# Embedding norm and first kv projection: single token tiles or pairs of them

## The chip, the cores and the metric

One Trainium2 chip, one of its cores. The metric is the device time of one execution in microseconds (us): lower is better. The engines are named by their work: TensorE (PE in the rows; PEld is its weight load), VectorE (DVE), ScalarE (ACT), GpSimd (POOL) and SyncE (SP), which only issues transfers. L128 is line 128 of the kernel before.

## What is computed

A two-layer decoder trunk over 512 tokens of 2048 features, all in fp32. What matters here is its start: the embedding is normalised over its features, and the first thing that layer 0 needs of it is the 320 columns of `w_in` that hold the compressed keys and values (256) and the shared rotary key (64).

```python
def layernorm(x, g, b):
    xf = x.astype(jnp.float32)
    mu = jnp.mean(xf, axis=-1, keepdims=True)
    var = jnp.mean(jnp.square(xf - mu), axis=-1, keepdims=True)
    y = (xf - mu) * lax.rsqrt(var + LN_EPS) * g + b
...
h = layernorm(x, emb_ln_g, emb_ln_b)
for l in range(DEPTH):
    h = hybrid_layer(h, positions, w_in[l], ...)
# in hybrid_layer: proj = x @ w_in, split into q_lat, kv_lat, k_rope and the gates
```

Everything behind this (attention, pooling, convolution, output projection, the second layer) is the same program before and after.

## The kernel before

**Numbers in two parts.** An fp32 product is made of three TensorE passes: each operand is split into a high part (a ScalarE copy to fp32r) and a low part (the VectorE difference, L79 to L81), and `mm3` (L99 to L103) adds high x high, high x low and low x high. So a k-step of a projection for one token tile is three matmuls, and each weight block must be split before it is used.

**The opening** is the block from L205 to L299. The 512 tokens are four tiles of 128; `xr[t]` holds tile t as four chunks of 128x512. `load_x` (L212) issues a tile's four chunks on SyncE's queue. `normalise(t, on_act)` (L219) does four `bn_stats`, then `ln_stats` (L119: aggregate, add epsilon, and the power -0.5 on GpSimd, L124), then an offset, and normalises the chunks, the first `on_act` of them on ScalarE (L227), the others on VectorE (L128).

`ln_to_x` (L133) turns a normalised tile: for every group of `nk` of the 16 column blocks it makes TensorE transposes into one PSUM bank (L142), applies gain and bias in the bank (L149 on VectorE for even groups, L151 on ScalarE for odd ones), and splits the bank into XH (ScalarE, L80) and XL (VectorE, L81). Four banks (`bankB`) go around. The first tile goes in groups of four blocks, the others in groups of two.

The weights come in six units: `load_w` (L233) loads 3 x 128 rows of the 320 columns (the last unit 128), `split_w` (L238) makes the high part on ScalarE (L241) and the low part on GpSimd (L244; unit 4 on VectorE, units 2 and 3 in one piece, the others in thirds). `kv_proj` (L198) then runs 16 k-steps for the given tiles into `kv_ps[t]`, one PSUM bank each.

**The order of the work.** Each engine runs its own queue in order. The code names the work tile by tile (L277 to L297): tile 0 is normalised and turned, with the weight splits in between; then the projection of tile t is woven with the turning of tile t + 1 at listed k-steps (`weave`, L156). A list scheduler takes this order as priorities and puts on each engine's queue what it expects to be ready, so the queues need not have the written order. SyncE's queue has x of tile 0, the gain and bias rows `ve`, the constants `ct` (with the identity for transposes), weight units 0 and 1, x of tile 1, unit 2, x of tile 2, units 3 to 5, x of tile 3, and the small vectors of later stages (L255 to L272). At most eight transfers are out at a time: a later one is issued when the one eight places ahead of it has landed. At the end `spill` (L130) stores the normalised tiles.

The next stage is the q projection of layer 0 (`in_steps`, L167): 128x512 matmuls whose weights are loaded and split in the same way. Behind its first four k-steps the four kv tiles, evacuated in the meantime (L361 to L370), are turned by transposes (L392).

Of the kernel before, what the change touches and what calls it, by code (L numbers as in the profile page):

```python
# [10 lines left out]
F32 = mybir.dt.float32  # L11
# [8 lines left out]
P = 128  # L20
# [4 lines left out]
NT = T // P  # L25
# [28 lines left out]
def hybrid_trunk(ctx: ExitStack, tc: tile.TileContext, consts, x, positions, emb_ln_g, emb_ln_b,  # L54
# [13 lines left out]
    def bankA():  # L68
        return psA.tile([P, 512], F32, name="bankA", tag="bankA")
# [7 lines left out]
    xn_dram = dram.tile([T, D], F32, name="xn_dram")  # L77

    def split(hi, lo, src):  # L79
        nc.scalar.copy(hi, src)  # L80
        nc.vector.tensor_sub(lo, src, hi.bitcast(F32))  # L81

    def unit(src, shape, into=None):

# [34 lines left out]
    def ln_stats(sp, stats):  # L119
        mv = sp.tile([P, 2], F32, name="mv", tag="mv", bufs=4)  # L120
        nc.vector.bn_aggr(mv, stats)
        rstd = sp.tile([P, 1], F32, name="rstd", tag="rstd", bufs=4)
        nc.vector.tensor_scalar(rstd, mv[:, 1:2], 1.0, LN_EPS, op0=ALU.mult, op1=ALU.add)
        nc.gpsimd.tensor_tensor(rstd, rstd, half[:, 0:1], op=ALU.pow)  # L124
        return mv[:, 0:1], rstd
# [4 lines left out]
    def spill(t, r):  # L130
        nc.sync.dma_start(xn_dram[t * P:(t + 1) * P, :], r.rearrange("p c n -> p (c n)"))

    def ln_to_x(ts, rs, vg, vb, nk):  # L133

        n = len(ts)
        w = n * P
        for s in range(KT // nk):
            ps = bankB()
            for j in range(nk):
                k = nk * s + j  # L140
                for i in range(n):
                    nc.tensor.transpose(out=ps[:, (n * j + i) * P:(n * j + i + 1) * P],  # L142
                                        in_=rs[i][:, k // 4, (k % 4) * P:(k % 4 + 1) * P], identity=ident)
            for j in range(nk):
                k = nk * s + j
                g, b = vec[:, vg + k:vg + k + 1], vec[:, vb + k:vb + k + 1]
                src = ps[:, j * w:(j + 1) * w]
                if s % 2 == 0:
                    nc.vector.tensor_scalar(src, src, g, b, op0=ALU.mult, op1=ALU.add)  # L149
                else:  # L150
                    nc.scalar.activation(src, src, AF.Identity, bias=b, scale=g)  # L151
            kq = slice(nk * s, nk * (s + 1)), slice(ts[0] * P, ts[0] * P + w)
            split(XH[:, kq[0], kq[1]], XL[:, kq[0], kq[1]], ps[:, :nk * w].rearrange("p (j q) -> p j q", j=nk))
            yield

    def weave(main, side, at):  # L156

# [51 lines left out]
    with tc.tile_pool(name="start", bufs=1, reuse_waits="tile") as sp:  # L209
        xr = M01 + [sp.tile([P, 4, 512], F32, name=f"xr{i}", tag=f"xr{i}") for i in range(2)]  # L210

        def load_x(t):  # L212
            src = x[0, t * P:(t + 1) * P, :].rearrange("p (c n) -> p c n", c=4)
            for c in range(4):
                nc.sync.dma_start(xr[t][:, c, :], src[:, c, :])

        st = [sp.tile([P, 4, 6], F32, name=f"stats{t}") for t in range(NT)]

        def normalise(t, on_act):  # L219
            for c in range(4):  # L220
                nc.vector.bn_stats(st[t][:, c, :], xr[t][:, c, :])  # L221
            mu, rstd = ln_stats(sp, st[t])
            o = sp.tile([P, 1], F32, name=f"off{t}")
            nc.vector.scalar_tensor_tensor(o, in0=mu, scalar=-1.0, in1=rstd, op0=ALU.mult, op1=ALU.mult)
            for c in range(4):
                if c < on_act:
                    nc.scalar.activation(xr[t][:, c, :], xr[t][:, c, :], AF.Identity, bias=o, scale=rstd)  # L227
                else:
                    norm_chunk(xr[t], c, mu, rstd)

        raws, us = [], []

        def load_w(u):  # L233
            src, n = kv_block(0, u)
            raws.append(sp.tile([P, 3 * KVN], F32, name=f"kvraw{u}"))
            nc.sync.dma_start(raws[u][:, :n * KVN].rearrange("p (a b) -> p a b", a=n), src)

        def split_w(u):  # L238
            n = kv_block(0, u)[1]
            d = dp.tile([P, 2, 1024], F32R, name="dunit", tag="dunit") if u < 5 else kvx  # L240
            nc.scalar.copy(d[:, 0, :n * KVN], raws[u][:, :n * KVN])  # L241
            step = n * KVN if u in (2, 3) else KVN
            for a in range(0, n * KVN, step):
                (nc.vector if u == 4 else nc.gpsimd).tensor_sub(  # L244
                    d[:, 1, a:a + step], raws[u][:, a:a + step], d[:, 0, a:a + step].bitcast(F32))
            us.append(tuple(d[:, i, :n * KVN].rearrange("p (a b) -> p a b", a=n) for i in range(2)))

        def to_vec(tl, n, at):
            vps = bankB()
            nc.tensor.transpose(out=vps[:, :n], in_=tl, identity=ident[:n, :n])  # L250
            nc.vector.tensor_copy(vec[:, at:at + n], vps[:, :n])

        ve = sp.tile([V_LG, P], F32, name="ve")
        vr = sp.tile([V_N - V_LG, P], F32, name="vr")
        load_x(0)  # L255
        for row, v in ((V_EG, emb_ln_g), (V_EB, emb_ln_b)):
            nc.sync.dma_start(ve[row:row + 16, :], v.rearrange("(a p) -> a p", p=P))
        nc.sync.dma_start(ct, consts)
        load_w(0)
        load_w(1)  # L260
        load_x(1)
        load_w(2)
        load_x(2)
        load_w(3)
        load_w(4)
        load_w(5)
        load_x(3)
        for row, v in ((V_LG, ln_g[0]), (V_LB, ln_b[0])):
            nc.sync.dma_start(vr[row - V_LG:row - V_LG + 16, :], v.rearrange("(a p) -> a p", p=P))
        for row, n, v in ((V_QG, 8, q_norm_g), (V_KG, 4, kv_norm_g), (V_PS, 8, pool_scale)):  # L270
            nc.sync.dma_start(vr[row - V_LG:row - V_LG + n, :], v.rearrange("l (a p) -> (l a) p", p=P))
        nc.sync.dma_start(vr[V_CW - V_LG:, :], conv_w.rearrange("l w (a p) -> (l w a) p", p=P))  # L272
        kv_ps = [bankA() for _ in range(NT)]
        def turn_x(t, nk):
            return ln_to_x((t,), xr[t:t + 1], V_EG, V_EB, nk)

        normalise(0, 3)  # L277
        to_vec(ve, V_LG, 0)
        first = turn_x(0, 4)
        next(first)  # L280
        split_w(0)
        next(first)
        next(first)
        for u in (1, 2, 3):
            split_w(u)
        next(first)
        split_w(4)
        normalise(1, 4)
        split_w(5)
        weave(kv_proj(us, kv_ps, (0,)), turn_x(1, 2), (11, 13) + 6 * (15,))  # L290
        normalise(2, 4)
        normalise(3, 0)
        weave(kv_proj(us, kv_ps, (1,)), turn_x(2, 2), tuple(range(5, 13)))
        weave(kv_proj(us, kv_ps, (2,)), turn_x(3, 2), (10, 12, 14) + 5 * (15,))
        to_vec(vr, V_N - V_LG, V_LG)
        for _ in kv_proj(us, kv_ps, (3,)):
            pass  # L297
        for t in range(NT):
            spill(t, xr[t])  # L299

# [556 lines left out]
```

## Time and profile before

| | |
|---|---|
| median of 3 runs | 1459.86 us (1459.64 to 1459.88) |
| profiled execution | 1459.91 us, span 1458.0 us |
| TensorE busy | 1435.6 us, 98% of the span |
| VectorE, ScalarE, GpSimd busy | 729.1, 561.8 and 108.0 us |
| share of TensorE in the chain that ended last | 98% |

The span runs from the first instruction to the last; the time has some 2 us around it. Times in the rows are us from the span's start. A timeline row gives the start, the time from the start of its first to the end of its last instruction, engine, line, operation, written tile and read tiles, shapes, how many were merged (x4), and in square brackets the idle time of the engine ahead of it and what ended it. Neighbouring instructions of an engine overlap at their ends, so the spacing of the starts is what one costs its engine, and the length is what the next engine waits. On TensorE the lengths are modelled; the starts are not.

### The profile page before, as it was taken

The numbers are of one execution on the slowest core, as the hardware profiler recorded it, in microseconds if no ns is written. First come the engines' busy times: TensorE is split into PE (matmuls) and PEld (weight loads), VectorE is DVE, ScalarE is ACT, GpSimd is POOL, SyncE is SP. The second block draws the span as 40 slices with busy tenths as digits, with TensorE's granted clock in tenths as the row PEclk, the third lists the DMA queues.
The fourth block names the chain that finished last, engine by engine and source line by source line (L and its number), as shares of the span: only waits on it lengthen the run. The fifth ranks groups of instructions, "written<-read, shape, count | busy, mean of one in ns | idle before, by whom it ended". The sixth has DMA issues, their size and how long they took to land.

```text
span 1458.0 us, 18179 instructions
## 1 busy us (share of the span) xinstructions
PE 1435.6 (98%) x7202; PEld 1226.9 (84%) x7202; DVE 729.1 (50%) x1244; ACT 561.8 (39%) x882; POOL 108.0 (7%) x130
## 2 busy tenths in 40 slices
PE   6999999999999999999999999999999999999997
PEld 6988888888888888888998888888888888888897
DVE  7745666553233257534573365666432423583336
ACT  7645566542222234222254365555322122432123
POOL 3011000012000000000001100000200000000004
PEclk9999999999999999999999999999999999999999
DMA  8532222133333347333523232232333333553333
GB/s 287 147 92 66 79 80 79 50 111 96 92 102 89 100 125 265 102 101 103 172 88 108 66 94 59 66 87 63 104 101 101 88 101 101 189 201 102 100 132 116
DMA packets 131104, 160.51 MB, mean 110 GB/s; under 512 B 13920, under 2 KB 109388, under 8 KB 127948
## 3 DMA queue, kind: packets, MB, share of 16 engines
q1 hardware_dynamic: 131020, 159.36, 36.1%
q8 instruction: 56, 0.92, 0.3%
q14 instruction: 28, 0.23, 0.0%
HBM read 146.76 MB, written 12.58 MB: 109 GB/s over the span
## 4 chain that ended last, share of the span: by engine, by line
PE 98%; ACT 0%; DVE 0%; DMA 0%; POOL 0%; issue 0%; SPq 0%; POOLq 0%; DVEq 0%; ACTq 0%
PE bankA L101 24%; PE bankA L102 24%; PE bankA L103 24%; PE bankB L103 7%; PE bankB L101 7%; PE bankB L102 7%; PE bankB L524 1%; PE bankB L142 1%; PE bankB L508 1%; PE bankB L507 1%; DMA M<-in_x_dram 0%; PE bankB L392 0%; POOL dunit L244 0%; ACT bankB L151 0%; ACT dunit L241 0%; DVE stats L221 0%
## 5 line engine op out<-in xcount | busy, mean ns | idle before, releaser
L81 DVE TENSOR_TENSOR dunit<-raw,dunit 128x1024 fp32r<-128x1024 f32 (+2 forms) x229 | 278.6, 1217 | 430.0 <-ACT dunit L80 430.0
L101 PE MATMUL bankA<-XH,dunit 128*128 128x512 f32 x1152 | 451.7, 392 | 0.0
L103 PE MATMUL bankA<-XH,dunit 128*128 128x512 f32 x1152 | 449.4, 390 | 0.0
L102 PE MATMUL bankA<-XL,dunit 128*128 128x512 f32 x1152 | 449.3, 390 | 0.0
L80 ACT CAST dunit<-raw 128x1024 fp32r<-128x1024 f32 (+2 forms) x229 | 237.3, 1038 | 540.4 <-PE bankA L103 407.9
L103 PEld LDWEIGHTS bankA<-XH,dunit 128*128 128x128 f32 x1152 | 216.3, 188 | 45.3
L101 PEld LDWEIGHTS bankA<-XH,dunit 128*128 128x128 f32 x1152 | 216.5, 188 | 42.5
L102 PEld LDWEIGHTS bankA<-XL,dunit 128*128 128x128 f32 x1152 | 216.5, 188 | 42.3
L101 PE MATMUL bankA<-dunit,XH 128*128 128x512 f32 (+1 forms) x376 | 139.2, 370 | 1.0 <-ACT XH L80 1.0
L102 PE MATMUL bankA<-dunit,XH 128*128 128x512 f32 (+1 forms) x376 | 138.2, 368 | 1.0 <-POOL dunit L244 1.0
L103 PE MATMUL bankA<-dunit,XL 128*128 128x512 f32 (+1 forms) x376 | 138.1, 367 | 0.0
L102 PE MATMUL bankB<-dunit,XH 128*128 128x512 f32 (+1 forms) x256 | 86.1, 336 | 0.0
L103 PE MATMUL bankB<-dunit,XL 128*128 128x512 f32 (+1 forms) x256 | 86.1, 336 | 0.0
L101 PE MATMUL bankB<-dunit,XH 128*128 128x512 f32 (+1 forms) x256 | 86.1, 336 | 0.0
L101 PEld LDWEIGHTS bankA<-dunit,XH 128*128 128x128 f32 x376 | 71.3, 190 | 11.5 <-ACT XH L80 1.7
L102 PEld LDWEIGHTS bankA<-dunit,XH 128*128 128x128 f32 x376 | 71.5, 190 | 11.3 <-POOL dunit L244 1.3
L103 PEld LDWEIGHTS bankA<-dunit,XL 128*128 128x128 f32 x376 | 71.3, 189 | 10.4 <-DVE XL L81 0.4
L102 PEld LDWEIGHTS bankB<-dunit,XH 128*128 128x128 f32 x256 | 48.6, 190 | 5.1
L103 PEld LDWEIGHTS bankB<-dunit,XL 128*128 128x128 f32 x256 | 48.6, 190 | 5.0
L101 PEld LDWEIGHTS bankB<-dunit,XH 128*128 128x128 f32 x256 | 48.6, 190 | 5.0
L514 ACT ACTIVATE scr<-bankB,st,r_q 128x128 f32<-128x128 f32 (+1 forms) x64 | 39.4, 617 | 34.5 <-DVE st L512 34.1
L101 PE MATMUL bankB<-qh,dunit 128*128 128x512 f32 x96 | 38.8, 405 | 0.0
(202 smaller groups left out, 1751.8 us busy)
## 6 DMA issues: line engine op xcount, KB each, us to landing
raw<-in_w_in_dram SPq DMA_DIRECT2D x144, 512.0 KB, 3.8
raw<-in_w_out_dram SPq DMA_DIRECT2D x64, 512.0 KB, 3.9
M<-xn_dram SPq DMA_DIRECT2D x8, 1024.0 KB, 4.9
xn_dram<-M SPq DMA_DIRECT2D x6, 1024.0 KB, 4.3
raw<-in_w_ukv_dram SPq DMA_DIRECT2D x8, 512.0 KB, 3.8
raw<-in_w_uq_dram SPq DMA_DIRECT2D x32, 128.0 KB, 2.3
out_dram<-M SPq DMA_DIRECT2D x16, 256.0 KB, 2.4
kvraw<-in_w_in_dram SPq DMA_DIRECT2D x5, 480.0 KB, 6.2
```

What stands on the lines that cost most here:

```text
L80: nc.scalar.copy(hi, src)
L81: nc.vector.tensor_sub(lo, src, hi.bitcast(F32))
L101: nc.tensor.matmul(acc, lhsT=ah, rhs=bh, start=first, stop=False)
L102: nc.tensor.matmul(acc, lhsT=ah, rhs=bl, start=False, stop=False)
L103: nc.tensor.matmul(acc, lhsT=al, rhs=bh, start=False, stop=last)
L142: nc.tensor.transpose(out=ps[:, (n * j + i) * P:(n * j + i + 1) * P], in_=rs[i][:, k // 4, (k % 4) * P:(k % 4 + 1) * P], identity=ident)
L507: nc.tensor.matmul(s[:, ks], lhsT=R[:, qs], rhs=KH[:, ks], start=False, stop=False)
L508: nc.tensor.matmul(s[:, ks], lhsT=R[:, qs], rhs=KL[:, ks], start=False, stop=True)
L514: nc.scalar.activation(pe[:, :W], s[:, :W], AF.Exp, bias=st[:, 1:2], scale=rs[:, qb:qb + 1], accum_out=st[:, 2:3])
L524: nc.tensor.transpose(out=pt[:, j * P:(j + 1) * P], in_=pe[:, j * P:(j + 1) * P], identity=ident)
```

## The change

Seven edits, all in the opening:

1. Tile 0's chunks 1 and 3, the gain and bias rows and the constants are issued on ScalarE's queue; tile 1 is loaded ahead of all weights.
2. TensorE multiplies a tile of zeros 22 times, does the one small transpose of the gain and bias, and multiplies zeros 14 times more.
3. Tiles are turned in pairs (0, 1) and (2, 3): a group is two column blocks of both tiles, four transposes into one bank, one affine of 128x256 on VectorE and one on ScalarE, a split of 128x512.
4. The projection runs for a pair at a time: 16 k-steps of six matmuls.
5. Tile 0 has chunks 0 and 1 normalised on VectorE, 2 and 3 on ScalarE; tile 1 and tile 3 all on VectorE; tile 2 has one on VectorE and three on ScalarE. The offset is made only where ScalarE needs it.
6. Ordering edges: tile 1's statistics start on VectorE behind tile 0's first normalised chunk, and so behind tile 0's offset; weight splits 1 to 3 follow the high parts of groups 0 to 2; tile 2's statistics follow the low part of group 3, splits 4 and 5 the power of tile 2; tile 3's statistics follow group 7.
7. All low parts of the weights are made on GpSimd, from unit 1 on in one piece.

`tc.issue_after(ins)` puts what is traced inside it behind `ins` on the queue of the engine of `ins`.

```diff
-    def ln_to_x(ts, rs, vg, vb, nk):
+    def ln_to_x(ts, rs, vg, vb, nk, both=False):
...
-                if s % 2 == 0:
+                if (j if both else s) % 2 == 0:
                     nc.vector.tensor_scalar(src, src, g, b, op0=ALU.mult, op1=ALU.add)
                 else:
                     nc.scalar.activation(src, src, AF.Identity, bias=b, scale=g)
...
             for c in range(4):
-                nc.sync.dma_start(xr[t][:, c, :], src[:, c, :])
+                eng = nc.scalar if t == 0 and c % 2 == 1 else nc.sync
+                eng.dma_start(xr[t][:, c, :], src[:, c, :])
+
+
+        zero = sp.tile([P, 512], F32R, name="zero")
+        nc.gpsimd.memset(zero.bitcast(F32), 0.0)
+        kv_ps = [bankA() for _ in range(NT)]
+
+        def warm(n):
+            for _ in range(n):
+                nc.tensor.matmul(kv_ps[3], lhsT=zero[:, 0:P], rhs=zero, start=True, stop=True)
...
+        def statistics(t):
+
+            with ExitStack() as order:
+                if t == 1:
+                    order.enter_context(tc.issue_after(started))
+                for c in range(4):
+                    nc.vector.bn_stats(st[t][:, c, :], xr[t][:, c, :])
+                mv = sp.tile([P, 2], F32, name=f"mv{t}")
+                nc.vector.bn_aggr(mv, st[t])
+                rstd = sp.tile([P, 1], F32, name=f"rstd{t}")
+                nc.vector.tensor_scalar(rstd, mv[:, 1:2], 1.0, LN_EPS, op0=ALU.mult, op1=ALU.add)
+            root = nc.gpsimd.tensor_tensor(rstd, rstd, half[:, 0:1], op=ALU.pow)
+            return (mv[:, 0:1], rstd), root
...
+        def normalise(t, c, mr, o=None):
+            if o is not None:
+                nc.scalar.activation(xr[t][:, c, :], xr[t][:, c, :], AF.Identity, bias=o, scale=mr[1])
+                return None
+            return nc.vector.tensor_scalar(xr[t][:, c, :], xr[t][:, c, :], mr[0], mr[1],
+                                           op0=ALU.subtract, op1=ALU.mult)
...
-            step = n * KVN if u in (2, 3) else KVN
+            step = n * KVN if u else KVN
             for a in range(0, n * KVN, step):
-                (nc.vector if u == 4 else nc.gpsimd).tensor_sub(
+                nc.gpsimd.tensor_sub(
...
         for row, v in ((V_EG, emb_ln_g), (V_EB, emb_ln_b)):
-            nc.sync.dma_start(ve[row:row + 16, :], v.rearrange("(a p) -> a p", p=P))
-        nc.sync.dma_start(ct, consts)
+            nc.scalar.dma_start(ve[row:row + 16, :], v.rearrange("(a p) -> a p", p=P))
+        nc.scalar.dma_start(ct, consts)
+        load_x(1)
         load_w(0)
         load_w(1)
-        load_x(1)
...
-        normalise(0, 3)
+        def turn_x(t):
+            return ln_to_x((t, t + 1), xr[t:t + 2], V_EG, V_EB, 2, True)
+
+        warm(22)
         to_vec(ve, V_LG, 0)
-        first = turn_x(0, 4)
-        next(first)
+        mr, _ = statistics(0)
+        o = offset(0, mr)
+        started = normalise(0, 0, mr).ins
+        for c in (2, 3):
+            normalise(0, c, mr, o)
+        normalise(0, 1, mr)
         split_w(0)
...
-        weave(kv_proj(us, kv_ps, (0,)), turn_x(1, 2), (11, 13) + 6 * (15,))
-        normalise(2, 4)
-        normalise(3, 0)
-        weave(kv_proj(us, kv_ps, (1,)), turn_x(2, 2), tuple(range(5, 13)))
-        weave(kv_proj(us, kv_ps, (2,)), turn_x(3, 2), (10, 12, 14) + 5 * (15,))
-        to_vec(vr, V_N - V_LG, V_LG)
-        for _ in kv_proj(us, kv_ps, (3,)):
-            pass
+        warm(14)
+        mr, _ = statistics(1)
+        first, second = turn_x(0), turn_x(2)
+        for i in range(4):
+            normalise(1, i, mr)
+            hi, lo = next(first)
+            if i < 3:
+                with tc.issue_after(hi.ins):
+                    split_w(i + 1)
+        with tc.issue_after(lo.ins):
+            mr, root = statistics(2)
+        for k, _ in enumerate(kv_proj(us, kv_ps, (0, 1))):
+            hi, lo = next(first, (hi, lo))
+            if k == 1:
+                with tc.issue_after(root.ins), tc.issue_after(hi.ins):
+                    split_w(4)
+                    split_w(5)
+                with tc.issue_after(lo.ins):
+                    o = offset(2, mr)
+                    for c in (1, 2, 3):
+                        normalise(2, c, mr, o)
+                    normalise(2, 0, mr)
+            if k == 3:
+                with tc.issue_after(lo.ins):
+                    mr, _ = statistics(3)
+                    for c in range(4):
+                        normalise(3, c, mr)
+            if k >= 10 and k % 2 == 0:
+                next(second)
+        for k, _ in enumerate(kv_proj(us, kv_ps, (2, 3))):
+            next(second, None)
+            if k == 8:
+                to_vec(vr, V_N - V_LG, V_LG)
```

## Rows read from the trace of the kernel before

**Rows 1.** The chain that ended last, up to 54 us: start, us, what.
```profile
2.12 5.28 DMA M<-in_x_dram
7.42 0.70 DVE stats L221
8.15 0.27 DVE mv L121
...
8.76 0.57 POOL rstd L124
...
9.54 0.82 ACT M L227
...
14.47 0.58 ACT XH L80
...
20.73 2.25 POOL dunit L244
```
**Rows 2.** Timeline of TensorE in the opening.
```profile
10.40 3.68 PE L142 MATMUL bankB<-ct,M 128*128 128x128 f32 x16 [1.93 <-ACT M L227]
15.11 0.64 PE L101 MATMUL bankA<-dunit,XH 128*128 128x320 f32 x1 [1.03 <-ACT XH L80]
...
18.30 0.47 PE L102 MATMUL bankA<-dunit,XH 128*128 128x320 f32 x1
18.56 0.47 PE L103 MATMUL bankA<-dunit,XL 128*128 128x320 f32 x1
...
21.54 0.45 PE L142 MATMUL bankB<-ct,M 128*128 128x128 f32 x2
23.02 0.41 PE L102 MATMUL bankA<-dunit,XH 128*128 128x320 f32 x1 [1.03 <-POOL dunit L244]
...
33.30 0.31 PE L101 MATMUL bankA<-dunit,XH 128*128 128x320 f32 x1
33.44 0.31 PE L102 MATMUL bankA<-dunit,XH 128*128 128x320 f32 x1
33.59 0.38 PE L142 MATMUL bankB<-ct,xr 128*128 128x128 f32 x2
33.73 0.39 PE L103 MATMUL bankA<-dunit,XL 128*128 128x320 f32 x1
33.96 0.38 PE L142 MATMUL bankB<-ct,xr 128*128 128x128 f32 x2
...
52.97 0.39 PE L101 MATMUL bankA<-XH,dunit 128*128 128x512 f32 x1
```
**Rows 3.** Windows: length, busy of PE, PEld, DVE, ACT, POOL (x), PEclk, DMA share, GB/s.
```profile
10.00:15.00 5.00, 3.68 (x16) 3.28 (x16) 3.44 (x9) 4.73 (x9) 2.28 (x3) 1.00 1.05 377
```
**Rows 4.** Timeline of SyncE's queue: the first tile's four issues.
```profile
0.73 1.82 SPq L215 DMA_DIRECT2D M<-in_x_dram  x4
```
**Rows 5.** View of tile M: landing of the eight x chunks of tiles 0 and 1.
```profile
DMA to landing us min/median/max: 3.6/4.3/6.6
```
**Rows 6.** Timeline of VectorE in the opening.
```profile
13.40 1.36 DVE L149 TENSOR_SCALAR bankB<-bankB,vec 128x128 f32<-128x128 f32 x4
...
17.81 1.26 DVE L81 TENSOR_TENSOR XL<-bankB,XH 128x512 fp32r<-128x512 f32 x2
...
20.55 1.28 DVE L221 BATCH_NORM_STATS2 stats<-xr 128x6 f32<-128x512 f32 x2
...
33.55 1.91 DVE L128 TENSOR_SCALAR xr<-xr,mv,rstd 128x512 f32<-128x512 f32 x4
```
**Rows 7.** Groups by shape, 0 to 50 us: busy us, mean ns | idle before.
```profile
L151 ACT ACTIVATE bankB<-bankB,vec 128x128 f32<-128x128 f32 x32 | 14.0, 448 | 3.1 <-PE bankB L142 2.9
...
L241 ACT CAST dunit<-kvraw 128x960 fp32r<-128x960 f32 x5 | 4.9, 984 | 0.0
```
**Rows 8.** Timeline of GpSimd in the opening.
```profile
12.72 7.21 POOL L244 TENSOR_TENSOR dunit<-kvraw,dunit 128x320 fp32r<-128x320 f32 x7 [3.41 <-ACT dunit L241]
19.89 0.56 POOL L124 TENSOR_TENSOR rstd<-rstd,half 128x1 f32<-128x1 f32 x1
20.73 2.24 POOL L244 TENSOR_TENSOR dunit<-kvraw,dunit 128x960 fp32r<-128x960 f32 x1 [0.28 <-ACT dunit L241]
```

More of the change, by code (lines that the diff above doesn't have):

```diff
@@ L79, in split @@
     def split(hi, lo, src):
-        nc.scalar.copy(hi, src)
-        nc.vector.tensor_sub(lo, src, hi.bitcast(F32))
+        return nc.scalar.copy(hi, src), nc.vector.tensor_sub(lo, src, hi.bitcast(F32))
     def unit(src, shape, into=None):
@@ L152, in ln_to_x @@
             kq = slice(nk * s, nk * (s + 1)), slice(ts[0] * P, ts[0] * P + w)
-            split(XH[:, kq[0], kq[1]], XL[:, kq[0], kq[1]], ps[:, :nk * w].rearrange("p (j q) -> p j q", j=nk))
-            yield
+            yield split(XH[:, kq[0], kq[1]], XL[:, kq[0], kq[1]],
+                        ps[:, :nk * w].rearrange("p (j q) -> p j q", j=nk))
     def weave(main, side, at):
@@ L214, in load_x @@
             for c in range(4):
-                nc.sync.dma_start(xr[t][:, c, :], src[:, c, :])
-        st = [sp.tile([P, 4, 6], F32, name=f"stats{t}") for t in range(NT)]
[L219 to L222, printed above, removed]
-            o = sp.tile([P, 1], F32, name=f"off{t}")
[L224 to L229, printed above, removed]
+                eng = nc.scalar if t == 0 and c % 2 == 1 else nc.sync
@@ new lines, in offset @@
+        def offset(t, mr):
+            o = sp.tile([P, 1], F32, name=f"off{t}")
+            nc.vector.scalar_tensor_tensor(o, in0=mr[0], scalar=-1.0, in1=mr[1], op0=ALU.mult, op1=ALU.mult)
+            return o
+        def normalise(t, c, mr, o=None):
[4 more added lines that the diff above has]
+                                           op0=ALU.subtract, op1=ALU.mult)
@@ L272, in hybrid_trunk @@
         nc.sync.dma_start(vr[V_CW - V_LG:, :], conv_w.rearrange("l w (a p) -> (l w a) p", p=P))
-        kv_ps = [bankA() for _ in range(NT)]
-        def turn_x(t, nk):
-            return ln_to_x((t,), xr[t:t + 1], V_EG, V_EB, nk)
-        normalise(0, 3)
+        def turn_x(t):
+            return ln_to_x((t, t + 1), xr[t:t + 2], V_EG, V_EB, 2, True)
+        warm(22)
         to_vec(ve, V_LG, 0)
-        first = turn_x(0, 4)
-        next(first)
-        split_w(0)
-        next(first)
-        next(first)
@@ L284, in hybrid_trunk @@
[L284 to L289, printed above, removed]
-        weave(kv_proj(us, kv_ps, (0,)), turn_x(1, 2), (11, 13) + 6 * (15,))
-        normalise(2, 4)
-        normalise(3, 0)
-        weave(kv_proj(us, kv_ps, (1,)), turn_x(2, 2), tuple(range(5, 13)))
-        weave(kv_proj(us, kv_ps, (2,)), turn_x(3, 2), (10, 12, 14) + 5 * (15,))
-        to_vec(vr, V_N - V_LG, V_LG)
-        for _ in kv_proj(us, kv_ps, (3,)):
-            pass
+        mr, _ = statistics(0)
```

## The prediction

> **What bounds the kernel now.** I read the chain of work that ended last first, in order of time. Up to 9.54 us it passes a DMA, VectorE, GpSimd and ScalarE [rows 1]; later nearly every piece is TensorE. So an edit of the opening is worth what it takes off the moment at which TensorE starts the next stage, the q projection. That moment is 52.97 us [rows 2]: the last 128x320 matmul is followed there by the first 128x512 one. I call it T. After T nothing is changed, and TensorE waits for nothing new there, so the time moves by what T moves.
>
> The chain's first pieces [rows 1] show what the opening waits for: the fourth x chunk, issued at 2.12 us, travels 5.28 us, and its bn_stats at 7.42 us, the power on GpSimd at 8.76 us and the normalisation at 9.54 us follow one another. Later the chain passes a 2.25 us GpSimd subtraction at 20.73 us. The stretch from 10 to 15 us [rows 3] says how full the others are: ScalarE 4.73 of 5 us, DMA share 1.05, VectorE 3.44.
>
> Then TensorE by instruction [rows 2]. In full swing a 128x320 matmul follows the last after 0.147 us (33.30, 33.44, 33.59), and a pair of transposes with one matmul takes 33.59 to 33.96, 0.37 us, so a transpose costs 0.11 us. The projection has 4 tiles x 16 x 3 = 192 matmuls, 28.2 us, and 64 transposes, 7.1 us: 35.3 us in all. From the first transpose, 10.40 us, to T it takes 42.6 us. The 7.3 us too much are: 16 transposes in 3.68 us, not 1.8 (1.9 lost); 1.03 us idle ahead of 15.11; 15 matmuls until 19.1 us at 0.267 us (18.30, 18.56), 1.8 lost; 1.03 us idle ahead of 23.02; the rest in small waits. 320 columns in 0.267 us are the 1.2 GHz level, in 0.147 us about the 2.4 GHz one, though the granted clock says 1.00 already from 10 to 15 us [rows 3]. What came before the rise was transposes alone, then some 4 us of matmuls.
>
> **The change, part by part.** It has two ends: TensorE at full clock from the start, and half as many, twice as wide, vector instructions; against that, both tiles of a pair must be normalised before the first projection matmul.
>
> *x on two queues.* The fourth chunk is issued with the second, at about 1.18 us instead of 2.12 [rows 1, 4]. That takes 0.94 us off 7.40: 6.5 us. The chunks' landing times run from 3.6 to 6.6 us [rows 5]; with the shortest the last would land at 4.8, and the later end is today's 7.4. I take 6.2, near the 6.5, with a little for ve and consts no longer standing behind it. The Trainium skill, "Trainium Kernel Development and Optimization", Key Constraints, says that issuing from several engines only saves the sequencer's issue time; by that rule the landing would be 6.5 us and all below 0.3 us later.
>
> *Tile 1 in time.* Landing of x0 to the first use of its statistics takes 7.40 to 9.54 today, of which 0.2 is the vec copy: 2.0 us [rows 1]. So VectorE normalises tile 0's two chunks from 8.2 to 9.1 us (four in 1.91, 0.46 each [rows 6]). Tile 1's four bn_stats, held behind the first of these, take 0.60 each (two in 1.28): 11.5. x1 now goes ahead of the weights; even issued only as x0's chunks land, at a median 4.3 us [rows 5], it is there by some 10 us, so VectorE, not the DMA, sets this step. Aggregate to power, 8.15 to 9.33 [rows 1], is 1.2 us: tile 1's first chunk is normalised from 12.7 to 13.2.
>
> *First matmul.* Four transposes (0.4), an affine, the 128x512 cast (0.58 [rows 1]). No 256-column affine stands in the trace: VectorE's 128-column one takes 0.34 (four in 1.36), two of them 0.68; a 512-wide subtraction takes 0.63 (two in 1.26) [rows 6], so it is between 0.34 and 0.68; I take 0.46, for both engines (ScalarE's 128-column one is 0.448 long [rows 7], the sum of two 0.9). First matmul: 13.2 + 0.4 + 0.5 + 0.6 + waits between engines of 0.2 = 14.9, against 15.11 today. Nothing is won up to here; but 16 transposes are done, and the clock is up.
>
> *The warm matmuls.* 36 of 512 columns: 0.43 us each at the low level (0.267 x 512/320), 0.23 at the high one. Begun at about 1.5 us, 4 us of them are slow (as from 15.11 to 19.1), so 22 end near 8.3 and the other 14 near 11.5, ahead of 12.7. They cost nothing as long as they end by then; all slow, they would end at 17.
>
> *TensorE's path.* 14.9 + 14.1 (96 matmuls) + 1.8 (16 transposes of the first pair's second half) = 30.8, with 1.2 for the low parts that come 0.6 behind the high ones, once at the start and once behind tile 2's statistics: 32.0.
>
> *VectorE's path to the second pair.* From 12.7: normalising tile 1, 4 x 0.46 = 1.9; eight groups x (0.46 + 0.63) = 8.7; tile 2's and 3's statistics, 2 x 2.7 = 5.4; offset and one chunk of tile 2, 0.6; tile 3's power, 0.7; its first chunk, 0.5: 17.8, so 30.5 if VectorE never idles. It must wait for casts on ScalarE, first of all the first; I give 2 us: 32.5. Then transposes, affine and cast as above: first matmul of the second pair at 34.1. This is later than TensorE's own 32.0 + 1.8 for 16 transposes, so VectorE's path ends last, by little. From there 14.1 + 1.8 us and 0.8 of small waits (as many as the 29.9 us from 23.02 to 52.97 had over its matmuls and transposes): **T = 50.8**, 2.2 us earlier.
>
> *Edits at nothing.* GpSimd has units 1 to 4 in whole pieces (2.25 us each [rows 1, 8]) against 2.6 us of matmuls for a unit: hidden; without cover, 0.1 to 2 us once. Unit 4's low part leaves VectorE for GpSimd, due only at k = 12. Behind T, tiles 2 and 3 are now evacuated together. TensorE needs them turned after 24 matmuls of 512 columns, 5.6 us at 0.235 (0.147 x 512/320); a tile takes a power (0.57) and four passes, each at most the 0.82 of a 512-wide one [rows 1]: 3.9 us, and the second 1.6 more: 5.5, covered; without cover, a few tenths. ScalarE's weight casts (0.98 [rows 7]) go one to a group, 0.98 + 0.46 + 0.5 = 1.9 against TensorE's 2.2 per group. The weights' issues on SP move behind x1, w0's to about 6.2 us, when x0 has landed; with a chunk's longest landing, 6.6 [rows 5], w0 is there at 12.8, cast (0.98) and its first third subtracted (0.83) by 14.6, ahead of 14.9, close. ScalarE's five DMA issues fall where it idles.
>
> Sum: the profiled execution took 1459.91 us (span 1458.0), the median is 1459.86, 0.05 less. 1459.9 - 2.2 = **1457.7**.
>
> **Rivals.** A measurement here can tell about 0.2%, 2.9 us, from no change: 1456.9 to 1462.8.
>
> *Both ends meet better* (0.25). VectorE loses no 2 us to casts, and x0 lands at 5.5, 0.7 earlier: VectorE's path is at the second pair at 34.1 - 2 - 0.7 = 31.4, TensorE's, without its 1.2 of waits for low parts, at 14.2 + 15.9 + 1.8 = 31.9. T = 31.9 + 15.9 + 0.8 = 48.6, the time 1455.5. For it: VectorE is idle for 1.56 of the 5 us from 10 to 15 us today [rows 3], so there is room to fill. Against: the first cast cannot come before VectorE has waited for it.
>
> *Power behind weights* (0.13). Tile 1's power is written behind w0's three GpSimd subtractions of 0.83 us. Today a power came right behind seven subtractions, at 19.89 [rows 8]. If w0's cast is done by 12 us, the power comes 2.5 us later: T = 53.3, time 1460.2. It decides whether the power starts before 13 us.
>
> *The clock falls back* (0.10). From 11.5 to 14.9 TensorE has only 16 transposes. In today's rows 16 transposes did not raise the clock [rows 2]. The price is today's own: 1.8 for 15 matmuls, 1.9 for transposes, less about 1 that VectorE's lateness hides: T = 53.5, time 1460.4. The Trainium skill, "TensorE: Matmul & The Clock Gate", Part 4, says that a transpose does not count as TensorE's work for the clock; by that rule the gap is as good as idle, and this rival's chance is not small. The trace agrees as far as it goes: 3.68 us of transposes were followed by 15 slow matmuls.
>
> *TensorE's queue holds the second pair too early* (0.07; the slower side). The second pair's first transposes are written behind k = 10. If they are queued there, k = 11 to 15 stand behind tile 3's normalisation at 32.5, while TensorE is at k = 10 at 14.9 + 8.8 + 1.8 + 1.2 = 26.7: it idles 5.8 us, then has 4.4 us of matmuls left. Second pair at about 38.5 with its transposes: T = 38.5 + 15.9 + 0.8 = 55.2, time 1462.1, and over 1462.8 with either rival above. Against: today tile 1's transposes, written behind k = 11, came at 21.54 behind k = 9 [rows 2], so the order is by readiness, not as written.
>
> **How the numbers follow.** The forecast has 0.45, its own range 1456.2 to 1459.3 (x0's landing 5.5 to 7.4, the affine 0.34 to 0.68 over 8 groups with half of it hidden, VectorE's wait 1 to 3). Faster by over 0.2%: the first rival, and 0.13 of the forecast's lower part: 0.38. Slower by over 0.2%: the last rival's upper half and pairs of the two before it, 0.07. The rest, 0.55, is within. Range for 8 in 10: 1455.0 to 1461.0.
>
> **What would show it.** Right: matmuls of 0.147 us spacing from the first; the first near 14.9 us; its 97th near 34; T near 50.8; TensorE idle 1 to 2 us between the pairs with VectorE at bn_stats just before. Wrong: tile 1's power behind w0's subtractions; spacing of 0.267 us behind 15 us; second-pair transposes with a long wait among the first pair's matmuls; or a stall after T, which I hold to be none.

## The result and the profile after

The median is 1468.58 us (1467.04 to 1469.92, six runs), against 1460.03 us for the kernel before on the same chip: ratio 1.0059, 95% interval 1.0048 to 1.0069. The change makes the kernel 0.6% slower, and the time is outside the range forecast (1455.0 to 1461.0).

The profiled execution has a span of 1467.1 us, 9.1 more than before. The q projection starts at 62.05 us, 9.08 later than in [rows 2], so the whole loss lies ahead of T. TensorE, to be set beside [rows 2]:

```profile
10.57 0.24 PE L273 MATMUL bankB<-ct,ve 32*128 32x32 f32 x1 [2.40 <-DMA ct<-in_consts_dram]
10.75 5.07 PE L224 MATMUL bankA<-zero 128*128 128x512 f32 x14
15.66 0.60 PE L141 MATMUL bankB<-ct,M 128*128 128x128 f32 x4
16.71 1.88 PE L141 MATMUL bankB<-ct,M 128*128 128x128 f32 x12 [0.45 <-DVE M L251]
20.72 0.41 PE L100 MATMUL bankA<-dunit,XH 128*128 128x320 f32 x1 [2.13 <-ACT XH L80]
...
42.51 1.53 PE L141 MATMUL bankB<-ct,xr 128*128 128x128 f32 x12 [1.71 <-DVE xr L251]
45.88 0.41 PE L100 MATMUL bankA<-dunit,XH 128*128 128x320 f32 x1 [1.84 <-ACT XH L80]
...
62.05 0.39 PE L100 MATMUL bankA<-XH,dunit 128*128 128x512 f32 x1
```

Three numbers divide the loss. The first product starts at 20.72 us (before 15.11; forecast 14.9): 5.6 lost. The second pair's first, the 97th of 192, starts at 45.88 (forecast 34.1), 25.2 behind the first where 19.2 were forecast. From there to T it takes 16.2 (forecast 16.7). So the late start and the way to the second pair are to be explained, and VectorE is what TensorE and ScalarE wait for in both. Its timeline, to be set beside [rows 6]:

```profile
10.85 0.19 DVE L274 COPY vec<-bankB 128x32 f32<-128x32 f32 x1 [3.16 <-PE bankB L273]
10.96 0.15 DVE L244 SCALAR_TENSOR_TENSOR off<-mv,rstd 128x1 f32<-128x1 f32 x1
11.03 1.00 DVE L251 TENSOR_SCALAR M<-M,mv,rstd 128x512 f32<-128x512 f32 x2
11.94 2.47 DVE L234 BATCH_NORM_STATS2 stats<-M 128x6 f32<-128x512 f32 x4
15.57 3.09 DVE L251 TENSOR_SCALAR M<-M,mv,rstd 128x512 f32<-128x512 f32 x3 [0.67 <-POOL rstd L239]
18.58 1.44 DVE L148 TENSOR_SCALAR bankB<-bankB,vec 128x256 f32<-128x256 f32 x3
...
31.66 2.21 DVE L244 SCALAR_TENSOR_TENSOR off<-mv,rstd 128x1 f32<-128x1 f32 x1 [0.20 <-POOL rstd L239]
...
38.29 2.46 DVE L234 BATCH_NORM_STATS2 stats<-xr 128x6 f32<-128x512 f32 x4
41.90 1.92 DVE L251 TENSOR_SCALAR xr<-xr,mv,rstd 128x512 f32<-128x512 f32 x4 [0.67 <-POOL rstd L239]
43.73 1.90 DVE L148 TENSOR_SCALAR bankB<-bankB,vec 128x256 f32<-128x256 f32 x4
```

Three things are to be seen. The copy of the constants stands ahead of tile 0's offset and waits until 10.85. The same operation has two speeds: two normalisations take 1.00 us at 11.03, three take 3.09 at 15.57, and the same 128x1 offset takes 0.15 at 10.96 and 2.21 at 31.66. And tile 3's statistics begin at 38.29 only, after which all four normalisations run ahead of the pair's first affine (43.73). ScalarE's queue has the reason for the first, GpSimd's timeline (beside [rows 8]) that for the second:

```profile
4.88 0.35 ACTq L281 DMA_DIRECT2D ct<-in_consts_dram  x1
```

```profile
15.50 2.88 POOL L267 TENSOR_TENSOR dunit<-kvraw,dunit 128x320 fp32r<-128x320 f32 x3
21.63 6.69 POOL L267 TENSOR_TENSOR dunit<-kvraw,dunit 128x960 fp32r<-128x960 f32 x3 [3.25 <-DMA xr<-in_x_dram]
31.08 0.55 POOL L239 TENSOR_TENSOR rstd<-rstd,half 128x1 f32<-128x1 f32 x1 [2.75 <-DVE rstd L238]
31.59 2.26 POOL L267 TENSOR_TENSOR dunit<-kvraw,dunit 128x960 fp32r<-128x960 f32 x1
```

Eight transfers are out by 2.7 us, so the issue of the constants waits on ScalarE until chunks of x land: issued at 4.88 us, they land 5.7 us later (the view of tile `ct`); before, they were issued at 3.5 and the transpose that needs them ran at 8.2. The slow instructions of VectorE begin within 0.1 us behind a GpSimd subtraction: 15.57 behind 15.50, 31.66 behind 31.59, and the offset ends at 33.87, where that subtraction ends (33.85).

The clock by windows (columns as in [rows 3]) is at its lower level, 1.2 GHz, in two stretches:

```profile
11.50:14.80 3.30, 3.30 (x9) 2.52 (x9) 3.23 (x8) 2.05 (x3) 0.00 (x0) 0.50 1.06 382
21.80:25.10 3.30, 3.30 (x15) 3.22 (x15) 1.24 (x2) 3.30 (x7) 3.30 (x2) 0.50 0.61 237
```

The first makes the 14 zero matmuls take 5.07 us; the second, behind the transposes and 2.13 us of idling, lies among the first products. Against this stood four theories: **A**, the constants' late landing; **B**, GpSimd's subtractions keep VectorE out; **C**, the clock; **D**, the order on VectorE between the pairs.

### The profile page after: what moved, and what is told of

Its sections match the earlier page's. It is cut to its first block, busy times and chain, and to the rows that moved or that the text cites. A ratio compares the mean times of both kernels' runs of the same rounds, so it can differ in the third digit from the quotient of the medians.

```text
span 1467.1 us, 18202 instructions
## 1 busy us (share of the span) xinstructions
PE 1445.7 (99%) x7238; PEld 1233.5 (84%) x7238; DVE 731.4 (50%) x1217; ACT 552.9 (38%) x848; POOL 109.8 (7%) x130
## 4 chain that ended last, share of the span: by engine, by line
PE 96%; DVE 1%; ACT 1%; issue 1%; POOL 1%; DMA 0%; POOLq 0%; DVEq 0%; ACTq 0%
PE bankA L102 24%; PE bankA L100 24%; PE bankA L101 24%; PE bankB L102 7%; PE bankB L100 7%; PE bankB L101 7%; PE bankB L567 1%; PE bankB L551 1%; PE bankB L550 1%; PE bankB L141 1%; DVE stats L234 0%; POOL dunit L267 0%; DMA M<-in_x_dram 0%; ACT bankB L150 0%; DVE M L251 0%
```

## The experiments

Those with one edit start from the changed kernel unless the kernel before is named. The time is the median of several executions, the ratio to the kernel before has its 95% interval behind it, and T and the rows are those of the one execution that was profiled. Such executions differ where nothing was edited: the copy of the constants, at 10.85 us in the changed kernel, ran at 9.51 to 10.29 in five experiments that leave the transfers and the work ahead of it as they are. So up to 1.3 us of an earlier first pair can be this.

**Without the low parts.** The low parts of the six weight units are left out (the high part stands in for them, with as many matmuls).

```diff
-            for a in range(0, n * KVN, step):
-                nc.gpsimd.tensor_sub(
-                    d[:, 1, a:a + step], raws[u][:, a:a + step], d[:, 0, a:a + step].bitcast(F32))
-            us.append(tuple(d[:, i, :n * KVN].rearrange("p (a b) -> p a b", a=n) for i in range(2)))
+            us.append(tuple(d[:, 0, :n * KVN].rearrange("p (a b) -> p a b", a=n) for i in range(2)))
```

> The changed kernel without GpSimd's subtractions: the high part of the weights is used for the low part too, so the low parts of the first kv projection are left out. Theory B (VectorE's SBUF-to-SBUF normalisations and the two-operand offset stand still while a GpSimd subtraction runs: 1.08 us each instead of 0.54, the offset 2.21 instead of 0.16): tile 1's three normalisations take 1.45 us instead of 3.09 and tile 2's offset 0.2, so the q projection starts 4 to 5 us earlier, near 57.5, time near 1464. Rival (the order of the queues alone makes the first pair late; GpSimd's work only stands beside it): the normalisations are as long as before, time 1468 to 1469.

1464.40 us, ratio 1.0032 (1.0021 to 1.0043), T at 57.05. VectorE's groups by shape up to 50 us, columns as in [rows 7]; first the changed kernel, then this one:

```profile
L80 DVE TENSOR_TENSOR XL<-bankB,XH 128x512 fp32r<-128x512 f32 x12 | 7.9, 678 | 2.9 <-ACT XH L80 2.9
L148 DVE TENSOR_SCALAR bankB<-bankB,vec 128x256 f32<-128x256 f32 x14 | 7.2, 543 | 2.5 <-PE bankB L141 2.5
L234 DVE BATCH_NORM_STATS2 stats<-M 128x6 f32<-128x512 f32 x8 | 5.0, 685 | 4.7 <-DMA M<-in_x_dram 4.7
...
L251 DVE TENSOR_SCALAR M<-M,mv,rstd 128x512 f32<-128x512 f32 x6 | 4.6, 812 | 0.7 <-POOL rstd L239 0.7
L251 DVE TENSOR_SCALAR xr<-xr,mv,rstd 128x512 f32<-128x512 f32 x5 | 3.1, 669 | 0.7 <-POOL rstd L239 0.7
L244 DVE SCALAR_TENSOR_TENSOR off<-mv,rstd 128x1 f32<-128x1 f32 x2 | 2.4, 1178 | 0.2 <-POOL rstd L239 0.2
```

```profile
L80 DVE TENSOR_TENSOR XL<-bankB,XH 128x512 fp32r<-128x512 f32 x15 | 10.0, 682 | 4.4 <-ACT XH L80 4.3
L148 DVE TENSOR_SCALAR bankB<-bankB,vec 128x256 f32<-128x256 f32 x16 | 8.3, 545 | 1.0 <-PE bankB L141 1.0
L234 DVE BATCH_NORM_STATS2 stats<-M 128x6 f32<-128x512 f32 x8 | 5.0, 685 | 5.0 <-DMA M<-in_x_dram 5.0
...
L251 DVE TENSOR_SCALAR M<-M,mv,rstd 128x512 f32<-128x512 f32 x6 | 3.0, 542 | 0.7 <-POOL rstd L239 0.7
L251 DVE TENSOR_SCALAR xr<-xr,mv,rstd 128x512 f32<-128x512 f32 x5 | 2.5, 542 | 0.7 <-POOL rstd L239 0.7
...
L244 DVE SCALAR_TENSOR_TENSOR off<-mv,rstd 128x1 f32<-128x1 f32 x2 | 0.3, 154 | 0.2 <-POOL rstd L239 0.2
```

B is shown, as much for what doesn't change: the operations that read PSUM (678 and 682 ns, 543 and 545) and the statistics (685 both times) run as fast beside GpSimd as alone. Only the normalisation from SBUF to SBUF (812 and 669 against 542) and the offset with two inputs in SBUF (1178 against 154) give way. That is 6 x 0.27 + 5 x 0.13 + 2 x 1.02 = 4.3 us of VectorE; T came 5.0 earlier. Not all of that is the subtractions': the constants were 0.6 earlier in this execution, and the granted clock was 1.00 from 6.7 us on, so the slow stretch at 21.8 is gone too. The Trainium skill, "SBUF — State Buffer", section "SBUF: two separate sides", says that VectorE's faster two-port modes and its operations on two SBUF inputs share a port pair with GpSimd, and that who starts first holds it for its whole instruction; the trace agrees, as the offset's end at 33.87 against the subtraction's at 33.85 shows.

**Constants on SyncE's queue**, behind tile 0 (theory A).

```diff
-            nc.scalar.dma_start(ve[row:row + 16, :], v.rearrange("(a p) -> a p", p=P))
-        nc.scalar.dma_start(ct, consts)
+            nc.sync.dma_start(ve[row:row + 16, :], v.rearrange("(a p) -> a p", p=P))
+        nc.sync.dma_start(ct, consts)
```

> The changed kernel with the gain, bias and constants back on SyncE's queue, right behind tile 0's chunks and ahead of tile 1; nothing else on any queue moves. Theory A (the vec copy, which waits for the late constants, holds VectorE's whole queue: tile 0's offset came at 10.96 us though its power was done at 8.41): the constants land near 8 us, the offset comes near 8.6, all of the first pair some 2.3 us earlier, and with the shorter gap among the zero matmuls the clock may hold; q projection starts near 59.5 us instead of 62.05, time near 1466. Rival (a later wait sets the end, the lock on VectorE or tile 1's landing): the offset comes early, the q projection not, time 1468 to 1469.

1467.74 us, ratio 1.0052 (1.0035 to 1.0068). The first product came at 18.65, 2.07 earlier, and the second pair's at 43.65, 2.2 earlier, but T at 61.24, only 0.8 earlier. A holds for the start; the forecast of T missed. The windows say where the rest was given back:

```profile
20.10:23.40 3.30, 3.30 (x16) 3.26 (x15) 1.26 (x3) 3.30 (x6) 3.30 (x2) 0.50 0.87 312
44.00:47.30 3.30, 3.30 (x15) 3.26 (x14) 2.21 (x4) 1.97 (x5) 0.00 (x0) 0.50 0.29 119
```

The second stretch at the lower clock now begins behind the gap between the pairs, where TensorE waits 1.84 us for a cast. From there to T nothing hides it: 17.6 us instead of 16.2.

**Without the zero matmuls** (theory C: `warm(22)` and `warm(14)` removed).

> The changed kernel without the 36 matmuls on zeros. Theory C (they bring nothing here: the granted clock falls to 0.5 from 11.47 to 14.88 and from 21.71 to 25.12 us all the same, and TensorE waits for VectorE): within 1.5 us of the changed kernel, 1467 to 1470. Rival (they are what keeps most of the first projection at the high level): as many slow matmuls and transposes as in the kernel before, 2 to 4 us slower, 1470.5 to 1472.5.

1468.96 us, ratio 1.0062 (1.0047 to 1.0077), T at 61.93, level with 62.05. Up to 24.41 us its 128x320 matmuls follow one another after 0.27 us, from 25.35 on after 0.15: TensorE came to the upper level at about 25.1 us, the moment at which the second slow stretch ends in the changed kernel. The zero matmuls bring nothing here.

**The kernel before with zero matmuls**, 22 at the start and 8 behind the constants' transpose.

```diff
...
+        warm(22)
         normalise(0, 3)
         to_vec(ve, V_LG, 0)
+        warm(8)
```

> The kernel before with 22 matmuls on zeros ahead of the vec transpose and 8 behind it, nothing else. If the clock, once up, holds through tile 0's transposes (theory of the prediction): 16 transposes at 0.11 instead of 0.23 us and the first 15 matmuls at 0.147 instead of 0.267, the q projection at 50 to 51 us instead of 52.97, time 1457 to 1458.5. If transposes leave it to fall again: a slow stretch of some 3.4 us later, in the first projection, and no gain, 1459.5 to 1460.5.

1461.40 us, ratio 1.0010 (1.0001 to 1.0019), T at 54.11, 1.1 later. TensorE, the window behind the transposes, and one row of VectorE:

```profile
10.90 1.91 PE L142 MATMUL bankB<-ct,M 128*128 128x128 f32 x16
15.36 0.41 PE L101 MATMUL bankA<-dunit,XH 128*128 128x320 f32 x1 [2.55 <-ACT XH L80]
```

```profile
16.30:19.60 3.30, 3.03 (x11) 3.04 (x12) 3.30 (x9) 3.20 (x8) 3.30 (x3) 0.50 1.07 367
```

```profile
20.77 2.22 DVE L232 SCALAR_TENSOR_TENSOR off<-mv,rstd 128x1 f32<-128x1 f32 x1
```

The transposes ran in 1.91 us, not 3.68, and TensorE then waited 2.55 us for ScalarE's cast; the clock fell all the same. The third row is theory B in the kernel before: with its work moved by a little, tile 1's offset falls beside a subtraction and takes 2.22.

**The kernel before with the clock held**: besides, two to five zero matmuls behind the transposes of each of tile 0's groups.

> The kernel before, with 22 zero matmuls ahead of the constants' transpose, 6 behind it, and two to five more behind the transposes of each group of tile 0, so that TensorE does not idle at all ahead of tile 0's products. If the clock was what held the old start, as the forecast took it: full clock from before 12 us on, q projection at 51.5 or earlier (before: 52.97), time 1458.4 or less. If GpSimd's low parts set the pace of the old first tile (2.25 us for each unit against 1.32 us that TensorE needs for one at full clock), TensorE waits there instead: q projection at 52.5 to 53.2, time 1459.4 to 1460.2, no change.

1461.22 us, ratio 1.0009 (1.0000 to 1.0018), T at 54.24. The granted clock is 1.00 from 6.8 us on, ahead of all transposes, and TensorE waits where it waited in [rows 2]; its row, and that of GpSimd:

```profile
23.65 0.41 PE L102 MATMUL bankA<-dunit,XH 128*128 128x320 f32 x1 [1.24 <-POOL dunit L255]
```

```profile
21.36 2.23 POOL L255 TENSOR_TENSOR dunit<-kvraw,dunit 128x960 fp32r<-128x960 f32 x1 [0.76 <-ACT dunit L252]
```

The second theory, that GpSimd sets the pace of the old first tile, came out: from the first product to the next tile's it takes 11.2 us (16.21 to 27.44) at the upper level, and 11.3 in the kernel before (15.11 to 26.41). It is somewhat worse than level, since the first product came 1.1 later and unit 3's low part 0.6 later than at 20.73 [rows 8].

**The changed kernel with the clock held**, two zero matmuls behind the transposes of groups 0 to 3.

> The changed kernel with two zero matmuls of 128x512 behind the transposes of each of groups 0 to 3 of the first pair, and nothing else. In the changed kernel the records show half clock at 11.47 to 14.88 and 21.71 to 25.12 us. Theory C (the clock costs a little, the rest is VectorE and its locks): the second stretch goes, the 1.5 us or so that its matmuls lost come back, the q projection starts near 60.5, time 1467.0. Rival (the clock is most of the loss): start of the q projection below 56, time below 1463. Rival (a stretch at half clock only moves to the gap between the pairs, where VectorE holds TensorE up): start of the q projection 61.5 to 62.5, time 1468 to 1469.

1466.72 us, ratio 1.0049 (1.0036 to 1.0062), T at 60.93:

```profile
21.80:25.10 3.30, 3.09 (x25) 2.82 (x23) 2.36 (x5) 3.30 (x8) 3.30 (x3) 1.00 0.40 142
44.10:47.40 3.30, 3.30 (x14) 3.26 (x15) 1.83 (x4) 1.41 (x3) 0.00 (x0) 0.50 0.12 45
```

T came 1.1 earlier, between the first theory (1.5) and the third (0): one stretch went, another came behind the gap. The second pair's first product came 2.7 earlier (43.20), and the constants, 1.3 earlier in this execution, are in that; so the stretch among the first products cost some 1.3 us at most. The other took 1.6 back (17.7 us from there to T instead of 16.2). The profiled execution was the slowest of five; the median is 1.9 us below the changed kernel's. The clock is a small part of the 9.1 us.

**Three orders, one by one** (theories B and D): tile 3's statistics behind group 5 rather than 7; tile 2's offset as the negated mean on VectorE and a product on GpSimd; unit 0's low part on VectorE.

```diff
                     normalise(2, 0, mr)
+                    mr, _ = statistics(3)
             if k == 3:
                 with tc.issue_after(lo.ins):
-                    mr, _ = statistics(3)
...
+            if t == 2:
+                root = nc.gpsimd.tensor_tensor(off2, off2, rstd, op=ALU.mult)
...
-                nc.gpsimd.tensor_sub(
+                (nc.gpsimd if u else nc.vector).tensor_sub(
```

> The changed kernel with tile 3's statistics behind group 5 of the first pair instead of group 7; its normalisation stays behind group 7. Theory D (the 5.5 us between the pairs, 40.38 to 45.88, is the chain statistics, power, normalisation, that was started only when the first pair's vector work had ended, at 38.29 us): bn_stats run while VectorE waits for ScalarE, tile 3 is normalised from 38.4 instead of 41.9, the second pair and the q projection start 3 to 3.5 us earlier, q projection near 58.8, time near 1465.3. Rival (those bn_stats only push group 6 and 7 back by as much as they win): within 1 us of the changed kernel.

> The changed kernel with tile 2's offset made on GpSimd right behind its power (VectorE negates the mean ahead of it), so that it cannot stand behind unit 4's subtraction. Theory B (2.05 of the offset's 2.21 us on VectorE are that subtraction's): ScalarE's three chunks start near 32.0 instead of 33.90, groups 6 and 7 and all behind them come 1.5 to 2 us earlier, q projection near 60.2, time near 1466.8. Rival (the offset was only as long as VectorE was free anyway, groups 6 and 7 wait for something else): less than 0.5 us.

> The changed kernel with weight unit 0's low part on VectorE instead of GpSimd, so that GpSimd is idle while tile 1 is normalised; VectorE has 1.4 us more to do. Theory B: the normalisations of tile 1 take 0.54 us instead of 1.08, and the first matmul comes 1 to 1.5 us earlier than 20.72, q projection near 60.8, time near 1467.3. Rival (VectorE's amount of work counts, not who runs beside it): 1.4 us more work on VectorE, first matmul near 21.5 to 22, no gain or a loss up to 1 us.

T was at 60.26, 61.30 and 61.61, that is 1.8, 0.75 and 0.4 earlier; the ratios 1.0058 (1.0040 to 1.0076), 1.0045 (1.0027 to 1.0063) and 1.0056 (1.0041 to 1.0072) don't tell these apart from the changed kernel, and all three fall short of their forecasts of T. Yet each edit does its part: the second pair's first product comes at 43.34, 43.56 and 43.85, 2.5, 2.3 and 2.0 earlier than 45.88, of which the constants' landing in these executions is 0.7 to 0.9. Then some of it is given back: from there to T it takes 16.9, 17.7 and 17.8 us instead of 16.2. In the second and third the lower clock comes behind the gap, as in the experiment with the constants (in the first its second stretch lies ahead of the gap, from 36.6 us):

```profile
44.50:47.70 3.20, 3.20 (x14) 3.16 (x14) 1.74 (x4) 1.38 (x3) 0.00 (x0) 0.50 0.10 41
45.60:48.80 3.20, 3.20 (x15) 3.11 (x15) 1.84 (x3) 0.58 (x3) 0.00 (x0) 0.50 0.02 5
```

What the third edit does, VectorE shows best, with GpSimd's row behind:

```profile
14.67 0.55 DVE L251 TENSOR_SCALAR M<-M,mv,rstd 128x512 f32<-128x512 f32 x1 [0.67 <-POOL rstd L239]
...
19.20 2.38 DVE L251 TENSOR_SCALAR M<-M,mv,rstd 128x512 f32<-128x512 f32 x1
```

```profile
19.04 4.62 POOL L267 TENSOR_TENSOR dunit<-kvraw,dunit 128x960 fp32r<-128x960 f32 x2 [4.41 <-ACT dunit L264]
```

With no subtraction beside it tile 1's first chunk takes 0.55; the fourth now meets unit 1's at 19.04 and takes 2.38.

**The four together**: constants on SyncE's queue and the three orders.

> The changed kernel with all four: constants on SyncE behind tile 0, unit 0's low part on VectorE, tile 2's offset on GpSimd, tile 3's statistics behind group 5. If the four losses are separate and lie one behind another on one path: 0.8 + 1.3 + 1.8 + 3.2 = 7.1 us, q projection near 55, time near 1461.5, still not ahead of the kernel before. If a loss that is gone lets the clock hold too, 1 to 2 us more. If TensorE's own path (matmuls and transposes from the first matmul) takes over, the sum falls short: 1463 to 1465.

1462.67 us, ratio 1.0020 (1.0010 to 1.0029), T at 55.08: as expected, 7.0 earlier, where the four alone give 3.8 in sum. The difference does not lie in waits ahead of the second pair: its first product comes at 38.57, 7.3 earlier, and with one edit alone it came 2.2, 2.5, 2.3 and 2.0 earlier, 9.1 in sum. It lies behind the gap. Here the granted clock is 1.00 from 20.1 us on, and from the second pair to T it takes 16.5 us, against 16.9 to 17.8 with one edit alone. Whether the clock falls at that place in every execution of those kernels no run shows.

**Repaired further**: the four; tile 1's offset on GpSimd and its chunks 1 and 3 normalised on ScalarE; the copy of the constants behind tile 0's normalisation; unit 0's low part behind group 0's affine; the zero matmuls of the clock experiment.

```diff
-            normalise(1, i, mr)
+            if i < 3:
+                normalise(1, i, mr, mr[2] if i == 1 else None)
             hi, lo = next(first)
+            if i == 1:
+                with tc.issue_after(hi.ins):
+                    normalise(1, 3, mr, mr[2])
+            if i == 0:
+                with tc.issue_after(affines[0].ins):
+                    low0()
```

> The four edits tried together before (constants on the sync queue, tile 3's statistics behind group 5, tile 2's offset on GpSimd, unit 0's low part on VectorE), and further: tile 1's offset on GpSimd too, the copy of the constants behind tile 0's normalisation, unit 0's low part behind the affine of group 0, tile 1's chunks 1 and 3 normalised on ScalarE, and two zero matmuls behind the transposes of groups 0 to 3. If locks, order and clock are the whole loss: first product at 15.5 to 16.5, first product of the second pair by 38 and less, q projection at 50.5 to 52.5, time 1457.0 to 1459.0, level with or faster than the kernel before (1459.9). If GpSimd's subtractions still cover the second pair's normalisation, or the clock falls elsewhere: q projection at 53.5 to 55, time 1460.5 to 1462.

1461.41 us, ratio 1.0012 (1.0003 to 1.0021): the best of the pairs, and still not level with the kernel before. T at 54.67 is in the rival's bounds, though not by its causes: no normalisation is slow (541 and 544 ns) and the clock is at its upper level from 6.7 us on. TensorE:

```profile
14.73 0.55 PE L143 MATMUL bankB<-ct,M 128*128 128x128 f32 x3 [1.61 <-DVE M L262]
...
17.97 0.30 PE L100 MATMUL bankA<-dunit,XH 128*128 128x320 f32 x1
...
32.55 0.41 PE L100 MATMUL bankA<-dunit,XH 128*128 128x320 f32 x1 [1.57 <-ACT XH L80]
...
38.16 0.42 PE L100 MATMUL bankA<-dunit,XH 128*128 128x320 f32 x1 [0.16 <-ACT XH L80]
```

Tile 0's offset is done at 8.5 us, yet the first product starts at 17.97, 2.9 later than before. TensorE must have tile 1 normalised too (14.73), and the first group's cast is done at 17.06; the other 0.9 goes to zero matmuls and transposes that stand ahead of the product on TensorE's own queue. From there to T it takes 36.7 us against 37.9 before: that is all the pair wins.

**Repaired once more**: tile 3's statistics behind group 6, its chunks 1 and 3 on ScalarE.

> The repaired version of the run before, with tile 3's statistics behind group 6 rather than group 5, and tile 3's chunks 1 and 3 normalised on ScalarE, by an offset made on GpSimd. There TensorE stood still for 1.57 us ahead of 32.55 us (an affine queued behind tile 3's statistics) and the second pair began at 38.16, with the q projection at 54.67. If that order was all that was left between the pairs: second pair at 36.5 to 37.2, q projection at 52.8 to 53.5, time 1459.3 to 1460.2, level with the kernel before; the rest against a start of 48.6 is that no product can begin before tile 1 is normalised too (first product 17.97 there against 15.11 in the kernel before). Rival (a stretch at half clock comes back, or GpSimd's last subtractions cover tile 3's normalisation): q projection at 54 to 56, time 1460.6 to 1462.5.

1463.24 us, ratio 1.0023 (1.0014 to 1.0032), T at 57.40: a miss, also for the rival's causes. VectorE, and ScalarE behind it:

```profile
33.20 0.69 DVE L80 TENSOR_TENSOR XL<-bankB,XH 128x512 fp32r<-128x512 f32 x1 [2.90 <-ACT XH L80]
33.80 2.46 DVE L239 BATCH_NORM_STATS2 stats<-xr 128x6 f32<-128x512 f32 x4
```

```profile
29.55 2.23 ACT L260 ACTIVATE xr<-xr,off,rstd 128x512 f32<-128x512 f32 x3 [2.25 <-POOL off L249]
31.68 0.97 ACT L155 ACTIVATE bankB<-bankB,vec 128x256 f32<-128x256 f32 x2
```

VectorE is free from 30.3 on, and group 6's cast still comes late, since ScalarE normalises three chunks of tile 2 (2.23 us) ahead of that group's affine: what held TensorE up at 32.55 was not tile 3's statistics alone. These, now behind that group's low part, start at 33.80 instead of 27.84, and the second pair with them at 41.22. No version beat the kernel before.

## Why the prediction was wrong

*T decides, and nothing happens behind it*: right (span 9.1 later, T 9.08).

*x on two queues*: right. Tile 0's power is at 7.85, 0.9 earlier than in [rows 1].

*"ScalarE's five DMA issues fall where it idles"*: this step failed. The cost lay not on ScalarE but with who waits for the fifth: issued at 4.88 us, behind the first landing, the constants came at 10.6, and the copy that waits for them stands on VectorE ahead of tile 0's offset. The offset could have come at 8.52, as in the repaired kernel; it came at 10.96, 2.4 us later than that and 2.8 later than forecast (0.6 to 1.3 less in other executions with the same queues).

*Tile 1 in time*: the term was right. From tile 0's first normalised chunk to tile 1's, 4.5 us were forecast, and 11.03 to 15.57 is 4.5.

*First matmul*, 2.2 us behind tile 1's first normalisation: it took 5.15 (15.57 to 20.72); without GpSimd's subtractions 3.5. So 1.6 is the subtractions', and 1.3 the two further normalisations that ran ahead of the affine and what waited behind them. The price of the affine, 0.46, was right (three in 1.44).

*"GpSimd has units 1 to 4 in whole pieces ...: hidden"*: the step that failed most. I asked whether the low parts come in time, not what they keep out while they run. No row of before had a normalisation beside a subtraction: the four of [rows 6] ran at 33.55, between GpSimd's works. The price, up to 5.0 us of T, is above my bound of 2.

*VectorE's path to the second pair*: 19.2 forecast, 25.2 measured. Without the subtractions, and without the slow stretch of the clock, it was 22.4; the other 3.2 is order and waits. I summed VectorE's work and 2 us of waits as if it could be done in any order, but tile 3's statistics stood behind group 7, whose low part waits for ScalarE's cast, itself behind tile 2's three chunks.

*The warm matmuls cost nothing*: nearly right (without them T is 61.93), but they end at 15.8, not 11.5, and *the clock* is not held by them. My rival "the clock falls back" came true as a mechanism; its place was right, its weight small: without that stretch T came 1.1 us earlier here, and in the kernel before, with the clock held, T came 1.3 later. There lay the deeper fault: I counted 3.7 us of the opening of before as lost to the clock, while GpSimd's low parts set the pace of that tile.

*Rivals*: the power did not stand behind weights (14.98 against 15.50). The second pair's transposes held TensorE back by 0.83 us only. My slower rival was a queue on TensorE; it should have been one on VectorE.

How the 9.1 us divide is not exact, as the parts don't add up: leaving the subtractions out gives 5.0, the four edits together 7.0, everything repaired 7.4; the 1.7 that remain are the pair's later start, 2.9, less the 1.2 won behind it. As 0.9 of the 2.9 is the repaired kernel's own zero matmuls and transposes, it stays open whether pairs could draw level.

## What to carry to other kernels

Before work is moved to GpSimd, or joined into longer pieces there, list what VectorE does from SBUF to SBUF in the same time: it may stand still for the whole piece, so the gain of an edit "in the shadow" is asked from both engines. When tiles are joined into pairs, the start waits for the second tile; count that first, against what the join saves. And read an edit's gain at the moment that it is meant to move as well as at the end: four edits each brought the second pair 2.0 to 2.5 us forward, in executions that differ by up to 0.9 anyway, and lost up to 1.6 of it behind that, mostly to the clock; together, 7.0 of 7.3 arrived at T.

## What the runs showed of the hardware that was not expected

A 128x1 operation took 2.21 us instead of 0.15, as long as the GpSimd subtraction beside it, while PSUM reads and statistics on the same engine were not touched. TensorE's clock fell to its lower level after transposes and a wait of about 2 us although matmuls had run before; where one stretch at that level was prevented, another could come behind the next gap.
